# Other places for slabs, convolution, rope tables and memory values in a two-layer encoder kernel

## The chip, the core and the metric

The kernel runs on one core of a Trainium2 chip. TensorE (PE) multiplies, VectorE (DVE) and ScalarE (ACT) work elementwise, GpSimd (POOL) and SyncE (SP) mostly start DMA transfers. The metric is the device time of one execution in microseconds (us), the median over runs.

## The reference

An encoder of two layers over 512 positions of width 2048, all in float32. Each layer normalises x, multiplies it by one wide matrix w_in, and cuts the product into the inputs of three groups of heads and a gate:

```python
q_lat, kv_lat, k_pe, gb, gc, xin, q_mem, gate = split_cols(h @ w_in[l])
q  = (rmsnorm(q_lat) @ w_uq[l])        # 8 heads, 128 + 64 wide; rope on the 64
kv = (rmsnorm(kv_lat) @ w_ukv[l])      # keys and values; k_pe is one shared rope key
a_out = softmax(q k^T * scale) v       # over all 512 positions
c_out = gb * conv3(gc * xin)           # depthwise, width 3, over positions
m_out = memory_attention(q_mem, mem_n @ w_mk[l], mem_n @ w_mv[l])   # 4 heads, 256 tokens
x = x + rmsnorm((concat(a_out, c_out, m_out) * silu(gate)) @ w_o[l])
```

The outputs must agree with this in float32 accuracy.

## The kernel before

**Precision.** Each float32 operand is split into a high part (a cast to a shorter format) and a low part (what the cast left out), and each product is three matmuls (L272 to L274: high·high, low·high, high·low; the line's first operand is a weight's wh or wl). A weight that arrives from DRAM as a 128x1024 tile `wr` is one *unit*: ScalarE casts wh (L189, 1.05 us), VectorE subtracts to wl (L190, 1.22 us).

**Fewer multiplications.** The products are arranged in the seven products P1 to P7 of Strassen's scheme. Some of their weights are sums of two blocks. Such a sum is made either on VectorE (L178), or by a DMA that adds a second block into a tile that holds the first; these accumulating loads are issued by GpSimd (L146, `more`), the plain ones by SP.

**Stages of a layer.** The input projection runs in groups, here called gs[0] to gs[4]: gs[2] gives the q and kv latents (416 columns to a matmul), gs[3] the memory queries qm and a part gm of the gate, gs[4] the gate parts ga0 and ga1. Then comes the mixer: rope of the queries, 16 iterations of memory heads, the MLA heads; then the output projection. A group is 28 steps; a step takes one unit and 12 matmuls.

**Turned rows.** Rows of gb, gc, qm, the latents and the gates are needed in another layout. They are transposed in blocks on VectorE (L767), written to DRAM (`sent`, L944) and read back in the other order (`fetched`, L951). `sent_rows` waits until the block is turned; `conv_back` fetches u (from gc) and y (from gb); `conv(l, c)` works on a quarter: ScalarE copies u and scales it (L973, L974), VectorE adds two taps (L975, L976) and multiplies into y (L978).

**Rope tables.** `tables` makes cosines and sines in layer 0, `tables_wide` spreads them into two scratch pieces, `tables_turned` transposes these on TensorE, copies the results to two more pieces (L396) and writes them to DRAM as `tabd`; `tables_fetch` reads them as `tab` before the rope. In the rope (`q_rope_steps`), four steps called first, second, both and away multiply by the tables (L1087 to L1097), split the result (`qrh` and the rest of `rm`) and write it as `qrd`; `fetch` reads it back as `QR`, used by the MLA scores (L1198).

**Buffers.** There are 8 raw tiles for wr, 3 for wh, 3 for wl, 4 scratch pieces of 128x512 (`scrap`), and 19 slabs of 128x2048 for longer-lived operands. A step that asks for a buffer waits until its last user is done.

**What sets the order.** The program is one list of steps, in the order of `put` and `add`. Ahead of a step's matmuls its loads and splits are emitted (`prep` runs two units ahead). Work that may be put off goes to a queue (`defer`), from which a step takes some when it has room (up to 2.5 us in hand); `until` empties the queue until something is there. On TensorE, SP and GpSimd the instructions run in the order written; on VectorE and ScalarE, from the middle of the first layer's first group on, the tile framework's scheduler decides the order. Each engine takes its instructions strictly in order, so an instruction that waits holds all behind it.

Of the kernel before, what the change touches and what calls it, by code (L numbers as in the profile page):

```python
# [6 lines left out]
F32R = mybir.dt.float32r  # L7
I32 = mybir.dt.int32
AF = mybir.ActivationFunctionType
# [7 lines left out]
NT = S // P  # L17
# [68 lines left out]
class Program:  # L86
# [23 lines left out]
    def add(self, fn, units=(), room=0.0, ahead=None):  # L110

        self.steps.append((list(units), fn, room, self.ahead if ahead is None else ahead))
# [115 lines left out]
def encoder(tc, x, xt, mem, memt, positions, columns, w_in, q_norm_g, w_uq, w_qr, kv_norm_g, w_ukv,  # L228
# [3 lines left out]
    nc = tc.nc  # L232
# [15 lines left out]
    pr = Program(nc, tc.keep_in_program_order, raw_p, hi_p, lo_p)  # L248
    add = pr.add

    G = {}
# [9 lines left out]
    def slab(name, dt=F32):  # L261
        return slabs.tile([P, D], dt, tag="slab", name=nm(name))
# [4 lines left out]
    def small(w=1, tag="st"):  # L267
        return stat.tile([P, w], F32, tag=tag, name=nm(tag))
# [7 lines left out]
    def split_to(hi, lo, src):  # L276
        nc.scalar.copy(hi, src)
        nc.vector.tensor_tensor(lo, src, hi.bitcast(F32), op=ALU.subtract)
# [633 lines left out]
            nc.gpsimd.dma_start(two[i], G["mTd"][2 * h + i])  # L912
        G.setdefault("mT", []).append(two)

    def mem_fetch():
        for n, k in (("Km", 4), ("Vm", 2)):
            t = slab(n, F32R)
            nc.gpsimd.dma_start(t, G[n + "d"])
            G[n] = t.rearrange("p (s i c) -> p s i c", s=2, i=k)


    def spots(t, c=4):

        return t.rearrange("q (p c k) -> q c p k", p=4, c=c)
# [30 lines left out]
    def sent_rows(name, C):  # L955
        def f():
            pr.until(lambda: C.get((name, "turned")) == NT)
            sent(name, C[name, "slab"])
        return f
# [10 lines left out]
    def conv(l, c):  # L970
        def f():
            u, y, w, g = scrap("u"), scrap("conv"), G[f"cw{l}"], G["ys"][2][:, c]
            nc.scalar.copy(by_tokens(u), spots(G["uw"])[:, c])  # L973
            nc.scalar.activation(y, u, AF.Copy, scale=w[:, 1, c:c + 1])  # L974
            nc.vector.scalar_tensor_tensor(y[:, 1:], u[:, :S - 1], w[:, 0, c:c + 1], y[:, 1:], op0=ALU.mult, op1=ALU.add)  # L975
            nc.vector.scalar_tensor_tensor(y[:, :S - 1], u[:, 1:], w[:, 2, c:c + 1], y[:, :S - 1],  # L976
                                           op0=ALU.mult, op1=ALU.add)
            nc.vector.tensor_tensor(g, by_tokens(y), g, op=ALU.mult)  # L978
        return f
# [38 lines left out]
    def k_rope(l, C):  # L1018
        m = scrap("kpm").rearrange("p (b t s i) -> p b t s i", b=2, t=NT, s=2)
        m1, m2 = m[:, 0], m[:, 1]  # L1020
        for t in range(NT):
            kp = C["lat"][t][:, O_PE:O_PE + ROPE].rearrange("p (s i) -> p s i", s=2)
            nc.vector.tensor_tensor(m1[:, t], kp, G["cos2"][:, t], op=ALU.mult)
            for s in range(2):
                nc.vector.tensor_tensor(m2[:, t, s, :], kp[:, 1 - s, :], G["sin2"][:, t, s, :], op=ALU.mult)
        kr = G["kvl"][:, 1024:1536].rearrange("p (g t j) -> p t g j", t=NT, j=32)
        nc.vector.tensor_tensor(kr[:, :, :2], m1, m2, op=ALU.add)
        nc.scalar.copy(kr[:, :, 2:], kr[:, :, :2])
        for h in (slice(0, 1024), slice(1024, D)):
            pr.defer(1.2, lambda h=h: nc.vector.transpose(G["ql"][:, h], G["ql"][:, h]))  # L1030
        pr.defer(1.8, lambda: nc.vector.transpose(G["kvl"][:, :1536], G["kvl"][:, :1536]))
        pr.defer(0.0, lambda: G.update(normalised=l))

    def latents_sent(l):
        pr.until(lambda: G.get("normalised") == l)
        sent("ql", G.pop("ql"))
        kv = G.pop("kvl")
        sent("kvl", kv[:, :1024], kv[:, 1024:1536])
# [4 lines left out]
    def latents_parts():  # L1043
        t, hi = G.pop("cqw"), slab("cqH", F32R)
        lo = t.bitcast(F32R)
        for h in (slice(0, 1024), slice(1024, D)):
            pr.defer(1.2, lambda h=h: split_to(hi[:, h], lo[:, h], t[:, h]))
        kt, khi = G.pop("ckw"), slab("ckvH", F32R)
        klo = kt.bitcast(F32R)
        for h in (slice(0, 768), slice(768, 1536)):  # L1050
            pr.defer(1.0, lambda h=h: split_to(khi[:, h], klo[:, h], kt[:, h]))

        def there():
            G["cq"] = spots(hi), spots(lo)
            kh, kl = (spots(a[:, :1536], 3) for a in (khi, klo))
            G["ckv"] = kh[:, :2], kl[:, :2]
            G["KA"], G["KB"] = kh[:, 2], kl[:, 2]
            G["latents"] = True
        pr.defer(0.0, there)

# [221 lines left out]

    def mixer(l, C, pair2, tail):

        add(tables_fetch)
        (p0, rotate0, fetch0), (p1, rotate1, fetch1) = (q_rope_steps(l, g) for g in range(2))
        put(p0)
        add(sent_rows("ga1", C))
        put(rotate0)
        sts = [{} for _ in range(4)]  # L1290
        qkv = qkv_steps(l, 0, sts[0])
        qkv[0] += (0.0, 1)
        qkv[2] += (0.0, 0)
        put(qkv[:1])
        its = [it for i in range(4) for it in mem_head(i)]
        m = len(its)
        between = {k: [s] for k, s in zip((2, 5, 8, 10, 12), qkv[1:])}
        between.setdefault(2, []).append((sent_rows("ga0", C), []))
        between.setdefault(11, []).append((gate_back(0, "ga0"), []))
        between.setdefault(6, []).append((fetch0, []))  # L1300
        between.setdefault(18, []).append((gate_back(1, "ga1"), []))
        between[m - 2] = [(lambda: pr.prep_next(), [])]
        for pair in range(4):
            for i in range(2):
                its += mla_head(2 * pair + i, sts[pair])
            nxt = tail if pair == 3 else spread(8, qkv_steps(l, pair + 1, sts[pair + 1]))
            if pair == 0:
                nxt = dict(zip((-1, 1, 3, 4, 6, 7), nxt_steps(nxt)))
            if pair == 2:
                nxt.update(pair2)  # L1310
            for k, v in nxt.items():
                between.setdefault(m + 8 * pair + k, []).extend(v)
        late = [(4, (tables_fetch, [])), (5, p1[0]), (6, p1[1])] + list(zip((6, 7, 8, 9), rotate1)) + [(11, (fetch1, []))]
        if l + 1 < depth:
            late += zip((12, 14, 16, 17, 18, 19, 20, 21), mem_turned_steps(l + 1))
        for k, s in late:
            between.setdefault(m + k, []).append(s)
        pipeline(its, between, m)
# [144 lines left out]
    def put(*passes):  # L1463
        for steps in passes:
            for s in steps:
                add(*s)
# [20 lines left out]
    for l in range(depth):  # L1487
        G["left"] = L = Left(l > 0)
        C, gs, owns = projection(l)
# [7 lines left out]
        if l == 0:  # L1497
            add(use)
            both = const.tile([P, 6], F32, name="factors")
# [34 lines left out]
        else:  # L1534
            put(ms[:1])
            add(use)
            for n in range(8):
                t, h = n // 2, n % 2
# [58 lines left out]
        put(*gs[l > 0][2:])  # L1597
        add(owns[2])
        steps = [s for passes in gs[2] for s in passes]
        put(steps[:6])  # L1600
        if l == 0:
            add(tables)
        put(steps[6:12])
        add(sent_rows(("gb", "gc")[l], C))
        put(steps[12:15])
        add(sent_rows(("gc", "gb")[l], C))
        put(steps[15:])
        add(owns[3])
        add(lambda l=l: latents_rows(l))
        steps = [s for passes in gs[3] for s in passes]  # L1610
        put(steps[:2])
        add(lambda l=l, C=C: latents_begin(l, C))
        put(steps[2:4])
        if l == 0:
            add(tables_wide)
        put(steps[4:8])
        add(lambda l=l, C=C: k_rope(l, C))
        add(conv_back)
        put(steps[8:12])
        if l == 0:  # L1620
            add(tables_turned)
        put(steps[12:14])
        add(conv(l, 0))
        put(steps[14:17])
        add(lambda l=l: latents_sent(l))
        put(steps[17:19])
        add(conv(l, 1))
        put(steps[19:22])
        add(conv(l, 2))
        put(steps[22:25])  # L1630
        add(conv(l, 3))
        put(steps[25:])
        add(owns[4])
        g4 = [s for steps in gs[4] for s in steps]
        put(g4[:2])
        add(latents_back)
        put(g4[2:6])
        add(sent_rows("qm", C))
        put(g4[6:8])
        add(sent_rows("gm", C))  # L1640
        put(g4[8:9])
        add(latents_parts)
        put(g4[9:14])
        add(lambda: G.update(qmw=fetched("qm", "QmL")))
        put(g4[14:19])
        add(qm_parts)
        put(g4[19:22])
        add(gate_back(3, "gm"))
        put(g4[22:26])
        add(mem_fetch)  # L1650
        put(g4[26:])
        add(lambda: pr.until(lambda: "Qm" in G and "cq" in G))
        G["left"] = Y = Left(False, True)
        g0, g1, gains, fetch = out_proj(l)
# [89 lines left out]
```

## Time and profile before

| | us |
|---|---|
| median of 3 runs (lowest, highest) | 1505.57 (1504.82, 1507.41) |
| the profiled execution | 1499.51 |
| its span in the trace | 1497.7 |
| TensorE busy | 1444.9 (96%) |
| VectorE busy | 1140.6 (76%) |
| ScalarE busy | 870.1 (58%) |
| GpSimd busy | 239.7 (16%) |

The mean granted clock of TensorE in that execution is 0.988. The page gives busy time by engine and by line; the timeline lists instructions with their start, their duration, and in brackets the engine's idle time before them with what ended it. TensorE's waits are grouped by the line that waited and by what it waited for. `<-` stands between what an instruction writes and what it reads. The profiled execution's own time is the one against which differences in the trace are counted.

### The profile page before, as it was taken

The numbers are of one execution on the slowest core, as the hardware profiler recorded it, in microseconds if no ns is written. First come the engines' busy times: TensorE is split into PE (matmuls) and PEld (weight loads), VectorE is DVE, ScalarE is ACT, GpSimd is POOL, SyncE is SP. The second block draws the span as 40 slices with busy tenths as digits, with TensorE's granted clock in tenths as the row PEclk, the third lists the DMA queues.
The fourth block names the chain that finished last, engine by engine and source line by source line (L and its number), as shares of the span: only waits on it lengthen the run. The fifth ranks groups of instructions, "written<-read, shape, count | busy, mean of one in ns | idle before, by whom it ended". The sixth has DMA issues, their size and how long they took to land.

```text
span 1497.7 us, 19187 instructions
## 1 busy us (share of the span) xinstructions
PE 1444.9 (96%) x6944; PEld 1225.9 (82%) x6944; DVE 1140.6 (76%) x1517; ACT 870.1 (58%) x1328; POOL 239.7 (16%) x248
## 2 busy tenths in 40 slices
PE   9999999969999999999999999999899999999997
PEld 8888889858878888788898888998787788878886
DVE  5899687767767788769788766758867776778687
ACT  7855343544557788654687433435555486776443
POOL 0031302111020010220220333021202000003101
PEclk9999999989999999999999999999999999999999
DMA  9999959597999193595986999595989985127983
GB/s 357 403 269 216 220 161 211 154 218 184 252 252 254 56 271 117 100 186 182 337 303 221 237 225 224 160 213 176 238 216 230 293 207 108 39 80 141 253 182 126
DMA packets 155038, 309.60 MB, mean 207 GB/s; under 512 B 11008, under 2 KB 35072, under 8 KB 151104
## 3 DMA queue, kind: packets, MB, share of 16 engines
q1 hardware_dynamic: 105472, 194.86, 43.0%
q0 software_dynamic: 49472, 113.52, 36.5%
q8 instruction: 54, 0.88, 0.3%
q14 instruction: 40, 0.33, 0.1%
HBM read 270.47 MB, written 37.88 MB: 206 GB/s over the span
## 4 chain that ended last, share of the span: by engine, by line
PE 63%; issue 16%; DMA 10%; DVE 5%; ACT 3%; POOL 2%; SPq 0%; POOLq 0%; DVEq 0%; ACTq 0%
PE P L273 14%; PE P L274 14%; PE P L272 14%; DMA wr<-in_w_in_dram 5%; POOL wr L146 2%; PE ptp L1217 2%; DVE wl L190 2%; DMA Km<-Kmd 1%; PE o L273 1%; ACT wh L189 1%; PE o L274 1%; PE o L272 1%; PE sc L272 1%; PE sc L273 1%; PE sc L274 1%
## 5 line engine op out<-in xcount | busy, mean ns | idle before, releaser
L189 ACT CAST wh<-wr 128x1024 fp32r<-128x1024 f32 (+2 forms) x436 | 443.6, 1023 | 442.7 <-PE P L274 313.8
L190 DVE TENSOR_TENSOR wl<-wr,wh 128x1024 fp32r<-128x1024 f32 (+2 forms) x436 | 513.3, 1185 | 229.8 <-ACT wh L189 225.4
L272 PE MATMUL P<-wh,S 128*128 128x512 f32 (+1 forms) x896 | 346.9, 387 | 23.5 <-ACT wh L189 23.5
L273 PE MATMUL P<-wl,S 128*128 128x512 f32 (+1 forms) x896 | 347.2, 388 | 7.3 <-DVE wl L190 7.2
L274 PE MATMUL P<-wh,S 128*128 128x512 f32 (+1 forms) x896 | 345.2, 385 | 0.0
L272 PE MATMUL P<-wh,A 128*128 128x512 f32 (+1 forms) x656 | 252.6, 385 | 0.0
L273 PE MATMUL P<-wl,A 128*128 128x512 f32 (+1 forms) x656 | 251.7, 384 | 0.0
L274 PE MATMUL P<-wh,A 128*128 128x512 f32 (+1 forms) x656 | 251.5, 383 | 0.0
L272 PEld LDWEIGHTS P<-wh,S 128*128 128x128 f32 x896 | 169.6, 189 | 55.8 <-ACT wh L189 25.4
L146 POOL DMA_DIRECT2D wr<-in_w_in_dram x108 | 130.2, 1210 | 495.3 <-DVE wl L190 314.7
L273 PEld LDWEIGHTS P<-wl,S 128*128 128x128 f32 x896 | 169.5, 189 | 41.3 <-DVE wl L190 11.4
L274 PEld LDWEIGHTS P<-wh,S 128*128 128x128 f32 x896 | 169.6, 189 | 30.5
L274 PEld LDWEIGHTS P<-wh,A 128*128 128x128 f32 x656 | 123.1, 188 | 22.3
L272 PEld LDWEIGHTS P<-wh,A 128*128 128x128 f32 x656 | 123.2, 188 | 21.9 <-ACT og L592 0.2
L273 PEld LDWEIGHTS P<-wl,A 128*128 128x128 f32 x656 | 123.2, 188 | 21.8 <-DVE wl L190 0.3
L146 POOL DMA_DIRECT2D wr<-in_w_o_dram x40 | 48.5, 1286 | 308.8 <-DVE wl L190 305.2
L1204 ACT ACTIVATE P<-sc,nm 128x512 f32<-128x512 f32 (+1 forms) x96 | 60.0, 625 | 26.2 <-DVE nm L1201 25.8
L178 DVE TENSOR_TENSOR wr<-wr,wr 128x1024 f32<-128x1024 f32 (+1 forms) x60 | 69.6, 1163 | 6.0 <-DMA wr<-in_w_in_dram 5.2
L1207 ACT ACTIVATE P<-P,rec 128x512 f32<-128x512 f32 (+1 forms) x96 | 62.5, 664 | 10.6 <-DVE rec L1206 10.6
L1201 DVE TENSOR_REDUCE nm<-sc 128x1 f32<-128x512 f32 (+1 forms) x96 | 56.7, 595 | 10.6 <-PE sc L1199 7.8
L1217 PE MATMUL ptp<-identr,P 128*128 128x128 f32 x320 | 46.0, 272 | 4.0 <-ACT P L1207 4.0
L1217 PEld LDWEIGHTS ptp<-identr,P 128*128 128x128 f32 x320 | 38.0, 140 | 10.3 <-ACT P L1207 4.4
(308 smaller groups left out, 2059.1 us busy)
## 6 DMA issues: line engine op xcount, KB each, us to landing
wr<-in_w_in_dram SPq DMA_DIRECT2D x128, 512.0 KB, 5.4
wr<-in_w_in_dram POOLq DMA_DIRECT2D x92, 512.0 KB, 8.1
wr<-in_w_o_dram SPq DMA_DIRECT2D x48, 512.0 KB, 6.6
wr<-in_w_o_dram POOLq DMA_DIRECT2D x40, 512.0 KB, 6.8
wr<-in_w_in_dram SPq DMA_DIRECT2D x32, 416.0 KB, 3.8
wr<-in_w_mk_dram SPq DMA_DIRECT2D x15, 512.0 KB, 8.6
wr<-in_w_mv_dram SPq DMA_DIRECT2D x15, 512.0 KB, 10.5
wr<-in_w_in_dram POOLq DMA_DIRECT2D x16, 416.0 KB, 7.8
```

The source lines that it names most:

```text
L146: engine.dma_start(dst, src, **kw)
L178: nc.vector.tensor_tensor(tiles[a], tiles[a], tiles[b], op=ALU.add)
L189: pin(nc.scalar.copy(hi[:, h], src[:, h]))
L190: pin(nc.vector.tensor_tensor(lo[:, h], src[:, h], hi[:, h].bitcast(F32), op=ALU.subtract))
L272: nc.tensor.matmul(ps, ah, bh, start=first, stop=False, **kw)
L273: nc.tensor.matmul(ps, ah, bl, start=False, stop=False, **kw)
L274: nc.tensor.matmul(ps, al, bh, start=False, stop=last, **kw)
L1201: nc.vector.tensor_reduce(nmax, ps, axis=AX.X, op=ALU.max, negate=True)
L1204: nc.scalar.activation(pt, ps, AF.Exp, bias=nmax, accum_out=tot)
L1207: nc.scalar.activation(pt, pt, AF.Copy, scale=rec)
L1217: nc.tensor.transpose(ps[:, k * P:(k + 1) * P], pt[:, k * P:(k + 1) * P], G["ident"])
```

## The change

Nothing is computed otherwise; steps are put elsewhere, and some storage is divided in another way.

- In gs[2], the slabs of gb and gc are written to DRAM at steps 7 and 8 (before at 12 and 15); the making of the rope tables follows step 8 (before 6).
- In gs[3], conv_back stands at step 5 (before 8), the four conv steps at 20, 22, 24, 26 (before 14, 19, 22, 25), the writing of the latents at 23 (before 17), with a wait for their normalisation put at 18.
- tables_wide and tables_turned go from gs[3] to steps 6 and 14 of gs[4]; tables_fetch goes ahead of the last step of gs[4].
- mem_fetch is divided: Km stays near the end of gs[4]; Vm is fetched after the first rope product, behind the tables.
- The key and value latents' high and low parts go into a slab of their own ("ckv"), the shared rope key's parts (KA, KB) stay in the fetched slab; they are split in pieces of 1024 and 512 columns, not 768 and 768.
- A one-column exponential is put on ScalarE ahead of the rope. The rope's last two steps go to iterations 1 and 3 of the memory heads, the fetch of QR from 6 to 7.

```diff
-    def mem_fetch():
-        for n, k in (("Km", 4), ("Vm", 2)):
+    def mem_fetch(n, k):
+        def f():
             t = slab(n, F32R)
             nc.gpsimd.dma_start(t, G[n + "d"])
...
-        kt, khi = G.pop("ckw"), slab("ckvH", F32R)
-        klo = kt.bitcast(F32R)
-        for h in (slice(0, 768), slice(768, 1536)):
-            pr.defer(1.0, lambda h=h: split_to(khi[:, h], klo[:, h], kt[:, h]))
+        kt, both = G.pop("ckw"), slab("ckv", F32R)
+        kv, kr = (kt[:, :1536].rearrange("q (p k) -> q p k", p=4)[:, :, o] for o in (slice(0, 256), slice(256, 384)))
...
+        pr.defer(1.2, lambda: split_to(khi, klo, kv))
+        pr.defer(0.7, lambda: split_to(ka, kb, kr))
...
-        add(tables_fetch)
...
-        put(p0)
+        put(p0[:1])
+        add(mem_fetch("Vm", 2))
+        put(p0[1:])
         add(sent_rows("ga1", C))
-        put(rotate0)
+        add(lambda: nc.scalar.activation(small(1, "ex"), C["ga0"][:, NT - 1][:, 0, :1], AF.Exp, scale=0.0))
+        put(rotate0[:2])
...
-        between.setdefault(6, []).append((fetch0, []))
+        for k, s in zip((1, 3), rotate0[2:]):
+            between.setdefault(k, []).append(s)
+        between.setdefault(7, []).append((fetch0, []))
...
-        put(steps[:6])
+        put(steps[:7])
+        add(sent_rows(("gb", "gc")[l], C))
+        put(steps[7:8])
+        add(sent_rows(("gc", "gb")[l], C))
         if l == 0:
             add(tables)
...
+        put(steps[2:5])
+        add(conv_back)
...
+        put(steps[18:20])
+        add(conv(l, 0))
...
-        add(conv_back)
-        put(steps[8:12])
-        if l == 0:
-            add(tables_turned)
-        put(steps[12:14])
-        add(conv(l, 0))
```

SP's order at the end of gs[2] in layer 0 (`wr` are plain loads, `sentgb` and `sentgc` the two written slabs). Before:

```order
L146 DMA wr68_1917<-in_w_in_dram 128x2x416
L146 DMA wr69_1971<-in_w_in_dram 128x2x416
L146 DMA wr70_2012<-in_w_in_dram 128x2x416
L146 DMA wr71_2053<-in_w_in_dram 128x2x416
L944 DMA sentgb_96_2100<-gb_52_867 128x4x512
L944 DMA sentgc_99_2175<-gc_31_651 128x4x512
```

Now:

```order
L146 DMA wr68_1917<-in_w_in_dram 128x2x416
L146 DMA wr69_1956<-in_w_in_dram 128x2x416
L945 DMA sentgb_93_1975<-gb_52_867 128x4x512
L945 DMA sentgc_94_1993<-gc_31_651 128x4x512
L146 DMA wr70_2010<-in_w_in_dram 128x2x416
L146 DMA wr71_2051<-in_w_in_dram 128x2x416
```

The two writes stand two loads earlier. VectorE's order around the convolution in gs[3] of layer 0 (`conv` and `y` belong to it; `wl` are the units' low parts). Before:

```order
L190 TENSOR_TENSOR wl122_2744<-wr73_2293,wh122_2743 128x1024
L767 STREAM_TRANSPOSE gm_100_2425<-gm_100_2425 128x16x32
L190 TENSOR_TENSOR wl123_2761<-wr85_2582,wh123_2760 128x1024
L975 SCALAR_TENSOR_TENSOR conv_132_2780<-u_131_2779,cols_100,conv_132_2780 128x511
L976 SCALAR_TENSOR_TENSOR conv_132_2780<-u_131_2779,cols_100,conv_132_2780 128x511
L975 SCALAR_TENSOR_TENSOR conv_136_2880<-u_135_2879,cols_100,conv_136_2880 128x511
```

Now:

```order
L190 TENSOR_TENSOR wl121_2699<-wr84_2538,wh121_2698 128x1024
L549 TENSOR_TENSOR gm_100_2425<-gm_100_2425,P2_121_2575 128x16x32
L767 STREAM_TRANSPOSE gm_100_2425<-gm_100_2425 128x16x32
L976 SCALAR_TENSOR_TENSOR conv_126_2867<-u_125_2866,cols_100,conv_126_2867 128x511
L767 STREAM_TRANSPOSE gm_100_2425<-gm_100_2425 128x16x32
L977 SCALAR_TENSOR_TENSOR conv_126_2867<-u_125_2866,cols_100,conv_126_2867 128x511
L976 SCALAR_TENSOR_TENSOR conv_128_2910<-u_127_2909,cols_100,conv_128_2910 128x511
L977 SCALAR_TENSOR_TENSOR conv_128_2910<-u_127_2909,cols_100,conv_128_2910 128x511
L976 SCALAR_TENSOR_TENSOR conv_132_2964<-u_131_2963,cols_100,conv_132_2964 128x511
L977 SCALAR_TENSOR_TENSOR conv_132_2964<-u_131_2963,cols_100,conv_132_2964 128x511
L979 TENSOR_TENSOR y_119_2565<-conv_126_2867,y_119_2565 128x4x128
```

The convolution began behind wl123 and begins now behind wl121; layer 1 moves in the same way, with wl353 and wl351. ScalarE's order at the start of the memory heads of layer 0 (Q is the memory query's split, `qrh` the rope's). Before:

```order
L189 CAST wh166_3663<-wr106_3532 128x1024
L189 CAST wh167_4059<-wr107_3550 128x1024
L277 CAST Q_168_3709<-qps_169_3710 128x512
L277 CAST qrh_167_3701<-rm_166_3695 128x1024
L1204 ACT_TABLE_LOAD
L1204 ACTIVATE P_172_3731,tot_173_3732<-sc_170_3725,nm_171_3729 128x256
```

Now:

```order
L189 CAST wh166_3661<-wr106_3527 128x1024
L1292 ACT_TABLE_LOAD
L1292 ACTIVATE ex_166_3695<-ga0_135_3055 128x1
L189 CAST wh167_4061<-wr107_3550 128x1024
L277 CAST Q_168_3703<-qps_169_3704 128x512
L277 CAST qrh_192_3786<-rm_167_3697 128x1024
L1206 ACTIVATE P_172_3725,tot_173_3726<-sc_170_3719,nm_171_3723 128x256
```

The load of the exponential's table stands two casts and a split earlier.

More of the change, by code (lines that the diff above doesn't have):

```diff
@@ L919, in mem_fetch @@
             G[n] = t.rearrange("p (s i c) -> p s i c", s=2, i=k)
+        return f
     def spots(t, c=4):
@@ L1047, in latents_parts @@
             pr.defer(1.2, lambda h=h: split_to(hi[:, h], lo[:, h], t[:, h]))
-        kt, khi = G.pop("ckw"), slab("ckvH", F32R)
-        klo = kt.bitcast(F32R)
-        for h in (slice(0, 768), slice(768, 1536)):
-            pr.defer(1.0, lambda h=h: split_to(khi[:, h], klo[:, h], kt[:, h]))
+        kt, both = G.pop("ckw"), slab("ckv", F32R)
+        kv, kr = (kt[:, :1536].rearrange("q (p k) -> q p k", p=4)[:, :, o] for o in (slice(0, 256), slice(256, 384)))
+        khi, klo = (both[:, o:o + 1024].rearrange("q (p k) -> q p k", p=4) for o in (0, 1024))
+        ka, kb = kt[:, 1536:].bitcast(F32R).rearrange("q (p k) -> q p k", p=4), kr.bitcast(F32R)
+        pr.defer(1.2, lambda: split_to(khi, klo, kv))
+        pr.defer(0.7, lambda: split_to(ka, kb, kr))
         def there():
             G["cq"] = spots(hi), spots(lo)
-            kh, kl = (spots(a[:, :1536], 3) for a in (khi, klo))
-            G["ckv"] = kh[:, :2], kl[:, :2]
-            G["KA"], G["KB"] = kh[:, 2], kl[:, 2]
+            G["ckv"] = spots(both[:, :1024], 2), spots(both[:, 1024:], 2)
+            G["KA"], G["KB"] = ka, kb
             G["latents"] = True
@@ L1599, in encoder @@
         steps = [s for passes in gs[2] for s in passes]
-        put(steps[:6])
+        put(steps[:7])
+        add(sent_rows(("gb", "gc")[l], C))
+        put(steps[7:8])
+        add(sent_rows(("gc", "gb")[l], C))
         if l == 0:
             add(tables)
[L1603 to L1607, printed above, removed]
+        put(steps[8:])
         add(owns[3])
@@ L1612, in encoder @@
         add(lambda l=l, C=C: latents_begin(l, C))
-        put(steps[2:4])
+        put(steps[2:5])
+        add(conv_back)
+        put(steps[5:8])
+        add(lambda l=l, C=C: k_rope(l, C))
+        put(steps[8:18])
+        add(lambda l=l: pr.until(lambda: G.get("normalised") == l))
+        put(steps[18:20])
+        add(conv(l, 0))
+        put(steps[20:22])
+        add(conv(l, 1))
+        put(steps[22:23])
+        add(lambda l=l: latents_sent(l))
+        put(steps[23:24])
+        add(conv(l, 2))
+        put(steps[24:26])
+        add(conv(l, 3))
+        put(steps[26:])
+        add(owns[4])
+        g4 = [s for steps in gs[4] for s in steps]
+        put(g4[:3])
+        add(latents_back)
+        put(g4[3:6])
+        add(sent_rows("qm", C))
         if l == 0:
             add(tables_wide)
-        put(steps[4:8])
-        add(lambda l=l, C=C: k_rope(l, C))
-        add(conv_back)
-        put(steps[8:12])
-        if l == 0:
-            add(tables_turned)
-        put(steps[12:14])
-        add(conv(l, 0))
[L1624 to L1638, printed above, removed]
         put(g4[6:8])
@@ L1642, in encoder @@
         add(latents_parts)
-        put(g4[9:14])
+        put(g4[9:11])
         add(lambda: G.update(qmw=fetched("qm", "QmL")))
-        put(g4[14:19])
+        put(g4[11:14])
+        if l == 0:
+            add(tables_turned)
+        put(g4[14:20])
         add(qm_parts)
-        put(g4[19:22])
+        put(g4[20:23])
         add(gate_back(3, "gm"))
-        put(g4[22:26])
-        add(mem_fetch)
-        put(g4[26:])
+        put(g4[23:26])
+        add(mem_fetch("Km", 4))
+        put(g4[26:27])
+        add(tables_fetch)
+        put(g4[27:])
         add(lambda: pr.until(lambda: "Qm" in G and "cq" in G))
```

## The prediction

> **What bounds the kernel now.** I read the page's busy shares first, then TensorE's waits, then every idle gap in TensorE's timeline, and only then the engine that each gap names.
>
> ```profile
> span 1497.7 us, 19187 instructions
> ...
> PE P L272 <- ACT wh L189: 23.5, 5, 13.0
> PE P L273 <- DVE wl L190: 7.2, 9, 1.2
> ...
> PE ptp L1217 <- ACT P L1207: 4.0, 2, 2.0
> ...
> PE sc L1198 <- DMA QR<-qrd: 0.3, 1, 0.3
> ```
>
> TensorE is busy for 96% of the span, so the span can only shrink where TensorE waits (columns: total us, times, longest) or runs at a lower clock. The waits on a weight's high part (wh) and low part (wl) are the larger part. The rows of the gaps (start, busy, what, idle time before it and its releaser):
>
> ```profile
> 264.35 0.71 PE L272 MATMUL P<-wh,S 128*128 128x416 f32 x1 [4.93 <-ACT wh L189]
> ...
> 265.40 0.71 PE L273 MATMUL P<-wl,S 128*128 128x416 f32 x1 [0.35 <-DVE wl L190]
> ...
> 336.14 0.80 PE L272 MATMUL P<-wh,S 128*128 128x512 f32 x1 [12.98 <-ACT wh L189]
> 337.94 0.80 PE L273 MATMUL P<-wl,S 128*128 128x512 f32 x1 [1.00 <-DVE wl L190]
> ...
> 436.57 0.50 PE L273 MATMUL P<-wl,S 128*128 128x512 f32 x1 [1.22 <-DVE wl L190]
> ...
> 464.58 0.44 PE L1217 MATMUL ptp<-identr,P 128*128 128x128 f32 x2 [2.00 <-ACT P L1207]
> ...
> 1009.96 0.46 PE L272 MATMUL P<-wh,S 128*128 128x416 f32 x1 [1.60 <-ACT wh L189]
> ...
> 1011.02 0.46 PE L273 MATMUL P<-wl,S 128*128 128x416 f32 x1 [0.60 <-DVE wl L190]
> ...
> 1069.79 0.80 PE L272 MATMUL P<-wh,S 128*128 128x512 f32 x1 [3.79 <-ACT wh L189]
> 1071.59 0.80 PE L273 MATMUL P<-wl,S 128*128 128x512 f32 x1 [1.00 <-DVE wl L190]
> ...
> 1075.37 0.40 PE L273 MATMUL P<-wl,S 128*128 128x512 f32 x1
> 1075.60 0.39 PE L274 MATMUL P<-wh,S 128*128 128x512 f32 x1
> ...
> 1145.89 0.50 PE L273 MATMUL P<-wl,S 128*128 128x512 f32 x1 [1.20 <-DVE wl L190]
> ...
> 1171.65 0.50 PE L273 MATMUL P<-wl,S 128*128 128x512 f32 x1 [0.99 <-DVE wl L190]
> ...
> 1199.70 0.44 PE L1217 MATMUL ptp<-identr,P 128*128 128x128 f32 x2 [2.00 <-ACT P L1207]
> ```
>
> They come in pairs, layer 0 and layer 1. **A/E**: the latents' group, 264.35 and 1009.96. **B/F**: the next group, gs[3], 336.14 and 1069.79. **C/H and G**: the last group, 436.57, 1171.65 and 1145.89. **D/I**: the first memory head, 464.58 and 1199.70. Matmuls of 512 columns start 0.23 apart (1075.37, 1075.60), so a unit of 12 is 2.7 us. After the long gaps TensorE also runs slowly; the columns below are the window, its length, busy us of PE, PEld, DVE, ACT, POOL, granted clock, DMA share, GB/s:
>
> ```profile
> 265.00:270.00 5.00, 4.65 (x15) 4.41 (x15) 2.81 (x4) 1.75 (x4) 0.00 (x0) 0.55 0.73 234
> ...
> 1070.00:1075.00 5.00, 4.00 (x9) 2.84 (x10) 4.97 (x6) 1.63 (x2) 2.44 (x2) 0.50 1.10 248
> ```
>
> Work of 4.00 us at clock 0.50 would have taken half, and 4.65 at 0.55 loses 2.1; with the edges I price one such stretch at 2.2 us. A, B and F have one each. So A costs 4.93 + 0.35 + 2.2 = 7.5, B 12.98 + 1.00 + 2.2 = 16.2, F 3.79 + 1.00 + 2.2 = 7.0, E 2.2, C 1.2, G 1.2, H 1.0, D and I 2.0 each: 40 us of the 1497.7.
>
> By the Trainium skill, "TensorE: Matmul & The Clock Gate", section "Part 1: The HAM clock gate", the clock halves after an idle window of about 3.4 us and returns after about as long under load. The trace agrees that 3.79 idle is followed by 0.50; working 3.4 us at half speed would make one stretch 1.7 us, an estimate from that page, and the sum below 1 us smaller.
>
> **A and E: two slabs written earlier.** The change issues the two writes "sent" (1 MB each) ahead of the last two loads of the group, not behind them.
>
> ```profile
> 231.57 0.46 SPq L944 DMA_DIRECT2D sentgb<-gb  x1
> ...
> 205.00:235.00 30.00, 30.00 (x159) 29.34 (x158) 28.48 (x61) 13.67 (x18) 1.18 (x1) 1.00 0.44 124
> 235.00:262.00 27.00, 24.42 (x131) 23.87 (x129) 16.79 (x35) 8.21 (x11) 8.33 (x7) 1.00 1.09 248
> ...
> DMA to landing us min/median/max: 6.1/7.8/10.8
> ```
>
> The DMA share is 0.44 until the writes start and full (1.09) after them, while GpSimd issues the accumulating loads (wr, L146) that finish the last weights. The last row is of those loads from 246.0 to 252.5: 6.1 to 10.8 us from issue to landing, the slowest being the last, for which A waits. Moved by two loads, the writes start near 222 and fall into the emptier stretch. Brought back to the median, the last load alone gains 10.8 − 7.8 = 3.0; those ahead of it on GpSimd's queue land sooner too. I take both gaps as gone: −7.5 and −2.2. Bounds: nothing gained (0), and all of it. Nothing queued on SP behind the writes is worse off: they need turned rows that are complete by then, and the two loads behind them are needed some 15 us later.
>
> **B and F: tables out, convolution earlier.** B is a wait on pieces (four scratch buffers):
>
> ```profile
> 326.51 0.62 ACT L973 COPY u<-u 128x512 f32<-128x512 f32 x1 [9.10 <-DMA tabd<-tab]
> ```
>
> The rope table's turned copies hold two pieces until written to DRAM. The change makes these copies in the last group, so 9.1 us go. But the four conv steps, though all are placed later in the program, stand two units earlier in the scheduled order of both VectorE and ScalarE: ahead of unit 122 (352 in layer 1), not 124 (354). All four ScalarE conv copies stand ahead of wh122. What they cost is read from F, where no table is in the way:
>
> ```profile
> L976 DVE SCALAR_TENSOR_TENSOR conv<-u,cols,conv 128x511 f32<-128x511 f32 x4 | 3.0, 748 | 0.1
> L975 DVE SCALAR_TENSOR_TENSOR conv<-u,cols,conv 128x511 f32<-128x511 f32 x4 | 3.0, 746 | 0.9 <-ACT conv L974 0.9
> L978 DVE TENSOR_TENSOR y<-conv,y 128x512 f32<-128x512 f32 x4 | 2.6, 685 | 0.0
> L178 DVE TENSOR_TENSOR wr<-wr,wr 128x1024 f32<-128x1024 f32 x2 | 2.4, 1218 | 0.0
> ...
> 1056.14 0.71 DVE L767 STREAM_TRANSPOSE gm<-gm 128x512 f32<-128x512 f32 x1
> ...
> 1056.26 0.63 ACT L800 ACTIVATE gm<-gm 128x512 f32<-128x512 f32 x1
> ...
> 1068.69 2.94 ACT L189 CAST wh<-wr 128x1024 fp32r<-128x1024 f32 x3 [1.57 <-DVE wr L178]
> ```
>
> In layer 1 the new block starts behind the first L767, at 1056.8. Ahead of the sum that releases wh352 stand six taps (4.5), the other L767 (0.7), three products (2.6 × 3/4 = 1.9) and that sum (1.2): 8.3, and some 0.7 of waiting on ScalarE for pieces (0.9 in the row): 1065.8. The cast takes 1.05, so wh352 is there at 1066.8. TensorE ran dry at 1069.79 − 3.79 = 1066.0 with units up to 353 ready; with units up to 351 it runs dry two units sooner, at 1060.6. The wait is 6.3, 1.0 more for wl behind the second sum as in F, and 2.2 of slow clock: 9.5 in each layer. Hence B −16.2 + 9.5 = −6.7 and F −7.0 + 9.5 = +2.5. Bounds for each new stall: 0, if the block fits ahead of need, and 16.2, B as it was.
>
> **C, H and G: order on VectorE.** H's row is 0.99 on wl, because a transpose stood ahead of it that waited for a SiLU (L800) queued behind the cast:
>
> ```profile
> 1168.17 1.05 ACT L189 CAST wh<-wr 128x1024 fp32r<-128x1024 f32 x1 [3.11 <-DMA wr<-in_w_in_dram]
> 1169.12 0.63 ACT L800 ACTIVATE ga<-ga 128x512 f32<-128x512 f32 x1
> ```
>
> In the new order both L800 stand ahead of that cast, so both transposes and the second half of qm_parts (now alone there) run while VectorE waits anyway: −1.2 and −1.0. In G one sum fewer (1.2) stands ahead of the wl: −1.2. The moved tables' transposes, writes and copies sit in slack of the last group, their DMAs on GpSimd's queue ahead of four accumulating loads; these could cost 1 to 2 us if the last of them landed later. Bounds for the three: −3.4 to +2; I take −3.4, since the 1 MB fetch of the memory values also leaves that place.
>
> **D and I: table load and rope.**
>
> ```profile
> 455.31 1.23 DVE L1087 TENSOR_TENSOR rm<-qr,tab 128x1024 f32<-128x1024 f32 x1 [2.23 <-DMA tab<-tabd]
> ...
> 460.29 1.05 ACT L277 CAST qrh<-rm 128x1024 fp32r<-128x1024 f32 x1 [1.26 <-DVE rm L1096]
> 461.36 1.28 ACT L1204 ACT_TABLE_LOAD   x1
> ```
>
> The first exponential stands behind the rope's split (1.05) and the load of its table (1.28). The dummy exponential takes the load ahead of wh167, where ScalarE idles; only copies and casts stand between it and the first real one, so no second load follows. The tables are fetched one unit earlier, ahead of the memory values: the 2.23 go, and the split runs some 2 us sooner. Together 1.28 + 2 exceed the 2.00 waited: −4.0 for both layers. If the cover failed (wh167 late), 1.28 would come back each time. TensorE then asks for QR sooner; its fetch waits for the low part of the rope, which still stands behind head work. The 0.3 may grow to 2.3 in a layer: I take +1.0 in all, bounds 0 to 4.
>
> By the Trainium skill, "ScalarE: Activation LUTs", section "What ACT_TABLE_LOAD costs", a switch is 2.66 us with a drain. The trace shows no drain ahead of the load (461.34 to 461.36) and 1.28 in all; at 2.66 the sum would be the same, since TensorE waited only 2.00.
>
> **Sum.** −7.5 − 2.2 − 6.7 + 2.5 − 3.4 − 4.0 + 1.0 = −20.3. The new key slab has the same number of elements to split (1536, in 1024 + 512): 0. The profiled execution took 1499.5 (span 1497.7 and 1.8 around it), 6.1 below the median of 1505.57; 1499.5 − 20.3 = 1479.2, and 1505.57 − 20.3 = **1485.3**, say 1485.
>
> **Rivals.**
> *Conv is free*: if the block is done before its units are needed, both new stalls vanish, 19 us more: 1466. For it: u and y come back sooner. Against: VectorE's order, and F's 3.79 with two more units ready. 0.12.
> *Loads stay late*: the writes only collide elsewhere, and A and E stay, +9.7: 1495. For it: the loads of the next group also start near 250. Against: 0.44 DMA share before. 0.15.
> *Conv waits for u (the slower side)*: the block's first instruction copies u, fetched from DRAM after its write; wh122 is behind it in ScalarE's queue.
>
> ```profile
> L951 SPq DMA_DIRECT2D u<-sentgc x8: 420/427/459, 300.9 to 1045.8; - x8
> ...
> DMA to landing us min/median/max: 5.0/6.2/7.3
> ```
>
> In layer 0 u's four issues began at 300.9 (0.42 each), so it had landed by some 310; the copy moves from 316.0 to about 311. If u came late, each microsecond would count twice; from 20.3/2 = 10 us late the kernel is slower, and at 12 it is 1509. Against: its fetch moves forward too. 0.07.
> *Gains return as other waits* (QR in place of P, accumulating loads in the last group) until under 3 us are left: 1505. 0.06.
>
> The forecast has 0.60, with its own range 1477 to 1493. Reaching to parts of the rivals, the range is 1468 to 1499. A measurement here tells 0.2% (3 us) from no change: faster 0.88, same 0.05, slower 0.07.
>
> **What would show it.** No gap near 264 and 1010, or under 1 us; near 330 and 1061 one gap of about 6 us on wh in both layers, with half clock behind it, and no wait on tabd; no gap on ptp; ACT_TABLE_LOAD at L1292 in idle time; wl right behind wh near 434 and 1168. A gap on u, on QR above 2.5 us, or gaps near 264 as before would show the terms wrong.

## The result, and the profile after

| | before | changed |
|---|---|---|
| median (us) | 1505.19 | 1486.43 |
| lowest, highest of 4 runs | 1502.02, 1507.41 | 1483.93, 1491.28 |
| profiled execution, its span | 1499.51, 1497.7 | 1484.13, 1482.3 |
| granted clock in it | 0.988 | 0.987 |

The ratio is 0.9881, with a 95% interval of 0.9846 to 0.9915: faster by 18.8 us in the medians, by 15.4 us in the two profiled executions. TensorE's waits in the changed kernel (total us, times, longest; left out are 1.4 us at the very start, as before, and three of 0.8 or less):

```profile
PE P L272 <- ACT wh L189: 18.6, 4, 6.2
PE P L273 <- DVE wl L190: 6.1, 9, 1.0
...
PE ptp L1219 <- ACT P L1209: 0.3, 2, 0.2
PE sc L1200 <- DMA QR<-qrd: 0.2, 1, 0.2
```

Before, the first row was 23.5 in five waits; now it is 18.6 in four, and two rows of before, both at the last MLA heads, are missing:

```profile
PE o L273 <- DVE PTl L278: 6.1, 2, 3.1
...
PE sc L272 <- ACT P L1204: 1.3, 2, 0.7
```

The gaps in TensorE's timeline from layer 0's gs[3] on, complete down to 0.6 us:

```profile
315.83 0.79 PE L272 MATMUL P<-wh,S 128*128 128x512 f32 x1 [6.24 <-ACT wh L189]
...
317.63 0.79 PE L273 MATMUL P<-wl,S 128*128 128x512 f32 x1 [1.01 <-DVE wl L190]
...
390.93 0.80 PE L272 MATMUL P<-wh,A 128*128 128x512 f32 x1 [3.08 <-ACT wh L189]
392.46 0.80 PE L273 MATMUL P<-wl,A 128*128 128x512 f32 x1 [0.74 <-DVE wl L190]
...
429.17 0.50 PE L273 MATMUL P<-wl,S 128*128 128x512 f32 x1 [0.63 <-DVE wl L190]
...
1051.72 0.80 PE L272 MATMUL P<-wh,S 128*128 128x512 f32 x1 [6.24 <-ACT wh L189]
1053.52 0.79 PE L273 MATMUL P<-wl,S 128*128 128x512 f32 x1 [1.00 <-DVE wl L190]
...
1127.42 0.56 PE L272 MATMUL P<-wh,A 128*128 128x512 f32 x1 [3.08 <-ACT wh L189]
1128.96 0.79 PE L273 MATMUL P<-wl,A 128*128 128x512 f32 x1 [0.97 <-DVE wl L190]
```

There is no gap near 264 or 1010 and none at the first memory head. Both layers have the same pair of gaps in gs[3], and both a pair in gs[4] that the kernel before had not. Behind all four TensorE is slow again (PEclk is the column after POOL's):

```profile
390.00:398.00 8.00, 6.34 (x15) 4.65 (x16) 6.54 (x8) 3.49 (x4) 0.77 (x1) 0.57 0.57 138
315.00:323.00 8.00, 6.17 (x15) 4.55 (x16) 7.58 (x9) 3.12 (x4) 3.66 (x3) 0.55 0.42 64
```

Busy time times one less the clock is 6.34 × 0.43 = 2.7 and 6.17 × 0.45 = 2.8 us lost.

The wh that ends the gap in gs[3] is cast as soon as VectorE, behind the taps of the convolution, has made its sum (ScalarE, layer 0):

```profile
314.73 2.94 ACT L189 CAST wh<-wr 128x1024 fp32r<-128x1024 f32 x3 [1.57 <-DVE wr L178]
```

In gs[2] the two writes start at 221.75, and the six accumulating loads from 237.8 to 249.4 land as the second row says; before, the same six were issued from 237.8 to 252.5 and took 6.1 to 10.8 us to land, in the median 8.4:

```profile
221.75 0.46 SPq L945 DMA_DIRECT2D sentgb<-gb  x1
...
DMA to landing us min/median/max: 6.4/6.6/7.4
```

So the last load is issued 3.1 us sooner and lands within 7.4 us, not 10.8. The DMA engines are not much emptier then: their share over 235 to 262 is 1.01, where it was 1.09.

ScalarE at the start of the memory heads: the table load lies in idle time, 8 us ahead of the first exponential, which follows the rope's split at once.

```profile
444.44 1.28 ACT L1292 ACT_TABLE_LOAD   x1
...
451.97 1.05 ACT L277 CAST qrh<-rm 128x1024 fp32r<-128x1024 f32 x1 [0.34 <-DVE wl L190]
452.92 0.47 ACT L1206 ACTIVATE P<-sc,nm 128x256 f32<-128x256 f32 x1
```

In gs[4] ScalarE shows why TensorE waits at 390.93:

```profile
379.85 1.05 ACT L189 CAST wh<-wr 128x1024 fp32r<-128x1024 f32 x1
386.52 0.59 ACT L578 COPY ga<-P 128x512 f32<-128x512 f32 x1 [5.62 <-PE P L274]
387.88 0.58 ACT L578 COPY ga<-P 128x512 f32<-128x512 f32 x1 [0.77 <-PE P L274]
388.36 1.05 ACT L277 CAST ckv<-ckvL 128x1024 fp32r<-128x1024 f32 x1
389.31 0.62 ACT L277 CAST ckvL<-ckvL 128x512 fp32r<-128x512 f32 x1
389.83 1.04 ACT L189 CAST wh<-wr 128x1024 fp32r<-128x1024 f32 x1
```

It idles 5.62 us for TensorE's results, since two copies of them stand ahead of the key latents' casts, and the next wh stands behind those. TensorE has by then used all it had in hand. The latents are not late: the last of their four transfers was issued at 366.7, and all landed within 8.5 us. In the kernel before, the casts stood ahead of the first of these copies:

```profile
391.37 1.05 ACT L189 CAST wh<-wr 128x1024 fp32r<-128x1024 f32 x1
392.32 1.57 ACT L277 CAST ckvH<-ckvL 128x768 fp32r<-128x768 f32 x2
...
400.75 0.59 ACT L578 COPY ga<-P 128x512 f32<-128x512 f32 x1 [2.41 <-PE P L274]
```

The list of the change leaves out one move that bears on this: `latents_back`, the step that fetches the latents, went from step 2 of gs[4] to step 3 (e3 takes that back).

### The profile page after: what moved, and what is told of

It is laid out like the page before. It is cut to its first block, busy times and chain, and to the rows that moved or that the text cites. A ratio compares the mean times of both kernels' runs of the same rounds, so it can differ in the third digit from the quotient of the medians.

```text
span 1482.3 us, 19184 instructions
## 1 busy us (share of the span) xinstructions
PE 1445.9 (98%) x6944; PEld 1227.9 (83%) x6944; DVE 1140.0 (77%) x1517; ACT 869.6 (59%) x1330; POOL 239.7 (16%) x248
## 4 chain that ended last, share of the span: by engine, by line
PE 75%; issue 9%; DVE 6%; DMA 5%; POOL 2%; ACT 2%; POOLq 0%; SPq 0%; DVEq 0%; ACTq 0%
PE P L273 17%; PE P L274 17%; PE P L272 17%; DMA wr<-in_w_in_dram 3%; PE ptp L1219 2%; DVE wl L190 2%; POOL wr L146 2%; PE o L273 1%; PE o L274 1%; PE o L272 1%; PE sc L274 1%; PE sc L273 1%; PE sc L272 1%; PE sc L1200 1%; PE qps L274 1%
## 5 line engine op out<-in xcount | busy, mean ns | idle before, releaser
L272 PEld LDWEIGHTS P<-wh,S 128*128 128x128 f32 x896 | 169.8, 189 | 44.1 <-ACT wh L189 13.3
L1203 DVE TENSOR_REDUCE nm<-sc 128x1 f32<-128x512 f32 (+1 forms) x96 | 56.7, 594 | 10.4 <-PE sc L1201 9.3
```

The costliest lines, as they stand in the source:

```text
L272: nc.tensor.matmul(ps, ah, bh, start=first, stop=False, **kw)
L1203: nc.vector.tensor_reduce(nmax, ps, axis=AX.X, op=ALU.max, negate=True)
```

## The experiments

Each edit is against the changed kernel or the kernel before; times are medians in us. Changed means 1486.4. The kernel before, run again beside each group of experiments, took 1504.3 (e1 to e4), 1502.6 (e5 to e8) and 1500.7 (e9 to e11); every ratio is to that.

**e1: conv where the scheduler had it before.** gs[3] as in the kernel before, without the tables' two steps:

```diff
-        put(steps[2:5])
+        put(steps[2:8])
+        add(lambda l=l, C=C: k_rope(l, C))
         add(conv_back)
...
-        put(steps[18:20])
+        put(steps[8:14])
         add(conv(l, 0))
```

> The changed kernel with gs[3] as before, except that the rope tables stay in gs[4]: conv_back at step 8, the conv steps at 14, 19, 22, 25. In the scheduled order the conv block then stands between wl123 and wl124 again, not between wl121 and wl122. Theory (the stall is set by the block's place in the engines' order, against the two units that TensorE has in hand): the gaps of 6.24 + 1.01 us at 315.83 and 1051.72 of the changed kernel shrink to the 3.79 + 1.00 that layer 1 of the kernel before shows, in both layers: about 5 us less than the changed kernel, some 1481 us. Rival (VectorE's whole work in the group sets it, or u's landing): the gaps stay at 6.2, 1486 us.

1480.8; ratio to before 0.9846 (0.9830 to 0.9863), against 0.9881 (0.9846 to 0.9915) of the changed kernel. The two intervals overlap, so it is the trace that tells:

```profile
318.91 0.80 PE L272 MATMUL P<-wh,S 128*128 128x512 f32 x1 [3.79 <-ACT wh L189]
...
1054.12 0.80 PE L272 MATMUL P<-wh,S 128*128 128x512 f32 x1 [3.79 <-ACT wh L189]
```

The gap is 3.79 in both layers, to the hundredth what layer 1 had before; the place of the block in the order sets it. The edit also moves conv_back and the latents' write, so their share is not separated, but neither shows as a wait.

**e2: conv broken up.** Each quarter can't start ahead of the unit prepared at its step:

```diff
                 outs[c] = (hi[:, :n], lo[:, :n])
+                self.last = hi
...
+            nc.scalar.copy(u[:, :1], pr.last[:, :1].bitcast(F32))
             nc.scalar.copy(by_tokens(u), spots(G["uw"])[:, c])
```

> The changed kernel, with each conv quarter tied to its step: before ScalarE copies u, it writes one column of the same piece from the wh prepared last, so the scheduler can't put the quarter ahead of that unit (eight copies of one column more, about 0.2 us each on ScalarE). Theory: the block is broken up, both gaps of 6.24 + 1.01 us and their half clock (2.2) go: 19 us less than the changed kernel, some 1467 us. Rival (VectorE has too little time in this group however the work lies): at most half of it goes, 1477 us or more, with new waits on wl between units 128 and 137.

1496.3, ratio 0.9946 (0.9927 to 0.9965): 10 us slower than the changed kernel. Theory and rival both failed. The gaps of 6.24 were gone, and a larger one came a little later; the second row is VectorE:

```profile
337.20 0.77 PE L273 MATMUL P<-wh,S 128*128 128x512 f32 x1 [11.61 <-DVE qm L550]
```
```profile
336.37 1.28 DVE L550 TENSOR_TENSOR qm<-gm,P 128x512 f32<-128x512 f32 x2 [7.47 <-DMA sentql<-ql]
```

VectorE is not short of time: it waits for a transfer. qm's first write waits for the write of ql to DRAM to land, which was issued at 328.7; so qm seems to get ql's slab here. In the changed kernel it can't: there ql is written only at 339.75, after qm's first write at 332.99, which does not wait. That it gets u's slab there, free because the conv block was done early, is argued and not shown. If so, the block that costs 6.24 us also frees a buffer in time.

**e3: latents fetched one step sooner.**

```diff
-        put(g4[:3])
+        put(g4[:2])
         add(latents_back)
-        put(g4[3:6])
+        put(g4[2:6])
```

> The changed kernel with one step moved back: latents_back at step 2 of gs[4], as before. It has a wait that the kernel before had not, 3.08 + 0.74 us at 390.93 and 3.08 + 0.97 at 1127.42, with half clock behind it. Theory (order: with the later fetch the scheduler puts the key latents' casts behind two copies of ga that wait for TensorE, and the next wh behind them): with the fetch one step sooner these casts stand ahead of wh146 and of the ga copies again, both waits and their half clock go, and 1.2 on a wl at unit 380 may come back: 10 us less than the changed kernel, some 1476 us. Rival (the new slab and the split in 1024 + 512 cause it): the wait stays at 3 us, 1486 us.

1471.9, ratio 0.9784 (0.9762 to 0.9807): 14.5 us less, more than the 10 expected. TensorE's waits on wh are now only the two of conv:

```profile
PE P L272 <- ACT wh L189: 12.5, 2, 6.2
PE P L273 <- DVE wl L190: 6.3, 8, 1.5
```

So the wait in gs[4] came from the fetch's step, not from the new slab. Its gaps (3.82 + 4.05) with the 2.7 of slow clock each make 13.3, close to the 14.5 of the medians (11.4 between the profiled executions); G's wait on wl came back in part (1.01 at 1126.79).

**e4: key latents as before**, in the changed kernel.

```diff
-        kt, both = G.pop("ckw"), slab("ckv", F32R)
+        kt, khi = G.pop("ckw"), slab("ckvH", F32R)
+        klo = kt.bitcast(F32R)
...
+        for h in (slice(0, 768), slice(768, 1536)):
+            pr.defer(1.0, lambda h=h: split_to(khi[:, h], klo[:, h], kt[:, h]))
```

> The changed kernel with latents_parts as before (ckvH in a slab, low parts and the rope key in the fetched slab, split in 768 + 768). Theory: the waits of TensorE at the last MLA heads (0.65 + 3.09 us at 605.78 and 0.66 + 3.02 at 1341.40 in the kernel before), which the changed kernel has not, went because the new slab changes the scheduled order there (the low parts PTl ahead of a split of S); without it the order is that of before, and 7.4 us come back: 1493 us. The wait of 3.08 us in gs[4] stays, since the casts still stand behind the ga copies. Rival (they went because QR, the exponentials or the memory heads are earlier): no such wait, 1486 us.

1496.9, ratio 0.9945 (0.9927 to 0.9963): 10.4 us more.

```profile
PE P L272 <- ACT wh L189: 18.6, 4, 6.2
PE o L273 <- DVE PTl L278: 6.1, 2, 3.1
...
PE sc L1199 <- DMA QR<-qrd: 2.3, 1, 2.3
...
PE sc L272 <- ACT P L1205: 1.3, 2, 0.6
```

The waits of the last heads are back (6.1 + 1.3), and the waits on wh unchanged. Beyond these there are the 2.3 on QR and slow clock behind the two PTl waits: it is 0.79 over 595 to 603 and 0.80 over 1340 to 1348, some 1.5 us each.

**e5: conv broken up, with the latents written and fetched sooner.** e2 and e3, with the quarters at 14, 18, 22, 26 and the write at step 17.

```diff
-        add(lambda l=l: pr.until(lambda: G.get("normalised") == l))
...
-        put(steps[22:23])
+        put(steps[14:17])
         add(lambda l=l: latents_sent(l))
```

> The changed kernel with three edits: conv quarters tied to their steps as in e2, now at 14, 18, 22, 26; the latents written at step 17 without the wait put ahead of it, as before; latents_back at step 2 of gs[4], as in e3. In e2 both conv gaps were gone, but a wait of 11.6 and 12.1 us on VectorE's qm (L550) came: qm took the slab of ql, which is free when its write to DRAM has landed, and that write was issued at 328.7. In the changed kernel qm takes u's slab, which the early conv block frees. Theory: with the write of ql issued near 301, as in e1, no wait is left in gs[3]; the 9.5 us of each layer go, 19 us less than e3's 1471.9: 1453 us. Rival (the spread conv makes the wait by filling VectorE): a wait of some 5 to 12 us stays on qm or wl in gs[3], and the time is 1465 us or more.

1468.7, ratio 0.976 (0.972 to 0.980). No wait on qm is left, which fits e2's cause; the quarters stand at other steps as well, so this edit does not separate the two. But 3.60 and 4.08 us stay in gs[3], on a wh; ScalarE's row:

```profile
338.45 1.04 ACT L189 CAST wh<-wr 128x1024 fp32r<-128x1024 f32 x1 [6.97 <-DMA wr<-in_w_in_dram]
```

It waits for an accumulating load, the last of the group, issued at 327.6 while SP, from 325.1 on, loads the next group's weights. With the conv stalls gone TensorE asks for that load sooner than the transfers bring it. The last six of these loads took 9.0 to 11.3 us to land, the eight from 301.5 to 330.8 in the changed kernel 6.5 to 9.3; that SP's loads slow them is argued, not shown. Of the 19 us some 3 were gained against e3, and the two intervals overlap.

**e6: the two writes alone**, in the kernel before.

```diff
-        put(steps[:6])
+        put(steps[:7])
+        add(sent_rows(("gb", "gc")[l], C))
+        put(steps[7:8])
+        add(sent_rows(("gc", "gb")[l], C))
```

> The kernel before with one part of the change: gb and gc written at steps 7 and 8 of gs[2], the making of the tables behind step 8. Theory: A (4.93 + 0.35 and 2.2 of slow clock at 264.35) and E (1.60 + 0.60 at 1009.96) go, nothing else: 9.7 us less than before, some 1495 us. Rival (the writes only collide elsewhere): the gaps stay or move to gs[2]'s other units, 1500 us or more.

1495.4, ratio 0.9940 (0.9917 to 0.9963): 7 us less than the 1502.6 of before in the same runs.

```profile
259.38 0.46 PE L272 MATMUL P<-wh,S 128*128 128x416 f32 x1 [0.67 <-ACT wh L189]
260.44 0.46 PE L273 MATMUL P<-wl,S 128*128 128x416 f32 x1 [0.60 <-DVE wl L190]
```

A went from 4.93 + 0.35 with slow clock to this, and E is gone; one of the loads still took 10.2 us to land. Its profiled execution was no shorter (1499.4), with new gaps of 0.78 + 0.76 at 940 and 0.6 more on B and on D; the timed runs carry the verdict.

**e7: the key latents alone**, in the kernel before.

```diff
-        kt, khi = G.pop("ckw"), slab("ckvH", F32R)
+        kt, both = G.pop("ckw"), slab("ckv", F32R)
```

> The kernel before with one part of the change: the key latents' slab and their split in 1024 + 512. The scheduled order of VectorE at the last MLA heads is then that of the changed kernel, and the casts in gs[4] do not stand behind the ga copies. Theory: the waits of 0.65 + 3.09 and 0.66 + 3.02 us at the last heads go, no wait of 3.08 comes: 7.4 us less than before, some 1497 us. Rival (those waits went for another reason): they stay, 1504 us.

1491.7, ratio 0.9912 (0.9877 to 0.9947): 11 us less than before in the same runs (7.1 between the profiled executions). No wait on PTl and none of 3.08 in gs[4]:

```profile
PE P L272 <- ACT wh L189: 23.2, 4, 13.5
PE P L273 <- DVE wl L190: 7.6, 9, 1.6
```

With e4 this shows from both sides that the slab's new layout takes the waits of the last heads away, by VectorE's order there, some 200 us later in the program. Before (VectorE in layer 0; PTl are the low parts for which TensorE waited, S a split for the output projection):

```profile
602.04 1.29 DVE L278 TENSOR_TENSOR PTl<-ptp,PTh 128x512 fp32r<-128x512 f32 x2 [0.85 <-PE sc L274]
603.25 1.28 DVE L278 TENSOR_TENSOR S<-y,S 128x512 fp32r<-128x512 f32 x2
604.45 1.28 DVE L278 TENSOR_TENSOR PTl<-ptp,PTh 128x512 fp32r<-128x512 f32 x2
```

In the changed kernel (e7's trace has the same order):

```profile
590.78 1.27 DVE L278 TENSOR_TENSOR PTl<-ptp,PTh 128x512 fp32r<-128x512 f32 x2
591.97 0.68 DVE L1203 TENSOR_REDUCE nm<-sc 128x1 f32<-128x512 f32 x1
592.56 1.28 DVE L278 TENSOR_TENSOR S<-y,S 128x512 fp32r<-128x512 f32 x2
```

S stood ahead of the second pair of PTl and stands now behind it; that is 1.28 of the 3.09 us waited. The first pair has moved further: it came behind the reductions `nm` at 594.55, 599.50 and 600.43, and now comes ahead of them, at 584.64. Why the scheduler decides so when a slab far ahead is laid out otherwise was not traced.

**e8: no early exponential**, in the changed kernel.

```diff
-        add(lambda: nc.scalar.activation(small(1, "ex"), C["ga0"][:, NT - 1][:, 0, :1], AF.Exp, scale=0.0))
```

> The changed kernel without the one-column exponential: the table is loaded (1.28 us) ahead of the first real exponential again. Theory (the 2.00 us of D and I went by both parts, table and rope): the load puts the first exponential later and 1 to 1.3 us come back at the first memory head in each layer: 2.5 us more than the changed kernel, 1489 us. Rival (the earlier rope alone was enough): no wait on P there above 0.5, 1486 us.

1485.9, ratio 0.9876 (0.9838 to 0.9915): in the timed runs no difference from the changed kernel. In the trace the gaps are back in part, and the profiled execution is 1.3 longer (1485.4 for 1484.1):

```profile
456.25 0.44 PE L1219 MATMUL ptp<-identr,P 128*128 128x128 f32 x2 [1.13 <-ACT P L1209]
```

In layer 1 it is the same 1.13. So of the 2.00 us of D about 1.0 belong to the early load and the rest, by subtraction, to the earlier rope; 2 us in all are too few for these runs to tell.

**e9: e1 and e3 together.**

> The changed kernel with the edits of e1 and e3 together. Theory (both stalls are of order, independent of each other): e1's gain (5.7 us) and e3's (14.5 us) add up: 1486.4 - 20.2 = 1466 us, with gaps of 3.79 + 1.00 in gs[3] of both layers and none of 3.08 in gs[4]. Rival (removing one stall lets transfers of the next one come late, as in e5): less than two thirds of e1's gain is left, 1468 us or more, with a wait on wh behind an accumulating load.

1465.1 (1464.7 to 1465.6), ratio 0.9764 (0.9749 to 0.9778): the lowest median, 21 us less than the changed kernel's. Since the kernel before was faster in these runs too, the ratios (0.9764 and 0.9881) make it 17.6.

```profile
317.71 0.50 PE L272 MATMUL P<-wh,S 128*128 128x512 f32 x1 [3.79 <-ACT wh L189]
319.51 0.80 PE L273 MATMUL P<-wl,S 128*128 128x512 f32 x1 [1.30 <-DVE wl L190]
...
1118.47 0.50 PE L273 MATMUL P<-wl,S 128*128 128x512 f32 x1 [1.00 <-DVE wl L190]
...
1190.50 0.47 PE L1200 MATMUL sc<-ckvL,QR 128*128 128x512 f32 x1 [1.56 <-DMA QR<-qrd]
```

In the trace the two gains add up: the gap in gs[3] is 3.79 in both layers, gs[4] has no wait on wh, and no wait of TensorE stands behind an accumulating load. In time they fit less closely: the ratios of e1 and e3 would add up to 0.9749, the lower end of the measured interval. Against e5 (0.976) no difference is shown: the compact conv block, at 3.79 us a layer, and the broken-up one, which meets the transfers, come out alike.

**e10: the tables alone**, in the kernel before: tables_wide and tables_turned at steps 6 and 14 of gs[4].

```diff
-        if l == 0:
-            add(tables_turned)
-        put(steps[12:14])
...
+        if l == 0:
+            add(tables_turned)
+        put(g4[14:19])
```

> The kernel before with one part of the change: tables_wide and tables_turned in gs[4], the conv steps left at 14, 19, 22, 25. Theory: B's wait for the pieces (9.1 of the 12.98 us) goes and layer 0 has then layer 1's gap, 3.79 + 1.00: 9.2 us less than before, some 1494 us. Rival (the fetch of u or the accumulating loads hold it as long): B stays above 8 us, 1499 us or more.

1493.6, ratio 0.9955 (0.9939 to 0.9971): 7 us less than before in the same runs (1500.7).

```profile
323.94 0.80 PE L272 MATMUL P<-wh,S 128*128 128x512 f32 x1 [3.79 <-ACT wh L189]
...
425.89 0.50 PE L273 MATMUL P<-wl,S 128*128 128x512 f32 x1 [1.88 <-DVE wl L190]
```

B is now layer 1's gap; on wl at 425.89 the wait of C grew by 0.66. That the tables did this is not shown: in layer 1, where none are made, H grew as well, to 1.88 (at 1163.45).

**e11: e9 with the rope undivided.**

```diff
-        put(rotate0[:2])
+        put(rotate0)
...
-        for k, s in zip((1, 3), rotate0[2:]):
-            between.setdefault(k, []).append(s)
-        between.setdefault(7, []).append((fetch0, []))
+        between.setdefault(6, []).append((fetch0, []))
```

> e9 with the rope's last two steps put ahead of the memory heads again and the fetch of QR at iteration 6, as before. Theory: the low part of the rope is then split ahead of head work, QR lands sooner and the 0.2 to 2.3 us that the runs wait for QR in layer 1 fall to 0.3, while the first memory head waits no more than 0.5 for P, since the table is loaded early: 1 us less than e9, 1465 us. Rival (the division is what took D and I away): up to 2 us come back on P in each layer, 1469 us.

1468.1, ratio 0.9790 (0.9770 to 0.9811): 3 us more than e9. In the trace the wait on QR is gone and two of 0.50 on the first head are there, so that place lost nothing; the same gap in gs[3] ended at 320.66, not at 317.71, behind steps in which the two kernels don't differ. The times speak for the divided rope, the traces don't; this stays open.

## Why the prediction was right, and where it was not

The forecast was 1485 in 1468 to 1499; measured were 1486.4. The total came out by terms that were right and two that were missing and in part cancel (+13.3 and −8.9), so that it came so close is partly luck.

- **A and E (−9.7): right.** No gap is left in either layer. The last load lands within 7.4 us, not 10.8, as was forecast (7.8); that it is also issued 3.1 us sooner was not. e6, alone: 7 us. The price is that of one trace: where gs[2] was left as before, A is 3.61 in e7 and 2.44 in e10, not 4.93.
- **B and F (−6.7 and +2.5): right, step by step.** 6.3 + 1.0 were forecast for each new stall, 6.24 + 1.01 and 6.24 + 1.00 measured. VectorE's order gave it; e1 shows that two units in that order are worth 6.24 − 3.79 = 2.5 us of gap a layer. The slow clock behind it was 2.8, not 2.2. e10 gives the tables' part. The rival "conv is free" fell with the trace, "conv waits for u" as well.
- **C, H and G (−3.4): wrong.** The waits named went (C to 0.63, H and G to nothing). What failed is that the prediction read gs[4] only at C, H and G: the fetch of the latents, moved from step 2 to step 3, was in no term, and ScalarE's order at the key latents' split was not compared. Two copies that wait for TensorE now stood ahead of those casts, and the next wh behind them: 3.82 and 4.05 us of gaps and some 2.7 of slow clock each, 13 us. The cause is the fetch's step (e3), and not the slab (e4, e7).
- **D and I (−4.0): right** (0.3 left), the load of the table in idle time as forecast; the division between load and rope is e8's, about half and half.
- **QR (+1.0): too high here** (0.2 for 0.3), though the same program's variants waited 0.7 to 2.3.
- **Missing: −8.9 at the last heads.** The waits there were 7.4 us, and the clock behind the one at 1341 was 0.79 over 8 us, another 1.5. The prediction's list of gaps leaves them out, though it says that every gap was read. It gave the new slab "0" because the number of elements is the same; e4 and e7 show that the slab takes these waits away, by VectorE's order.

Put together in gaps and slow clock: −9.7, −6.7 + 2.5 (+ 1.2 for the slower clock), −2.8, −3.7, −8.9, +13.3 is −14.8, beside −15.4 in the two traces; the rest is in gaps below 0.6 and in the first 300 us, which differ by 1 to 3 us between runs of programs that are equal there.

## What to carry to other kernels

Where a scheduler sets an engine's order, a moved step must be followed to its new neighbours on every engine, and each engine's order compared in all of the program: the two largest terms that were missing were both visible there before any run. A stall that looks like too much work can be order (e1, e3), and breaking the work up seems to have taken away a buffer that the compact block freed (e2). Stalls hide each other: with one gone, the transfers behind it were the next limit (e5).

## What was not expected of the hardware

- The length of a gap alone did not decide whether slow clock followed. In the kernel before, the clock stayed at 1.00 over 605 to 613, behind 3.09 us of waiting, and was 0.79 over 1340.5 to 1348.5, behind 3.02. It was 0.57 over 390 to 398 in the changed kernel, behind 3.08; 0.57 over 261 to 269 in e10, behind 2.44; and 0.79 over 941 to 949 in e6, behind 0.78 + 0.76. Nor does it always begin with the first matmul: behind 3.79 us in e9 the first took 0.50 us (317.71 and 1041.97), as behind short waits, where others took 0.80.
- One and the same kind of accumulating load took 6.1 to 10.8 us in layer 0's gs[2] beside the two writes; after they were moved, 6.4 to 7.4 in the changed kernel, but up to 10.2 in e6.
